# Five PSUM tiles from another set of banks, a recurrence in smaller steps, and memory attention ending later, in a one-core decoder step

## The chip, the cores and the metric

The kernel runs on one core of one Trainium2 chip. The core has five engines with queues of their own: PE multiplies matrices (PEld loads its weights), DVE and ACT work element by element, POOL issues a few transfers, and SP issues nearly all others. Each engine takes its instructions in the order in which the program wrote them into its queue; an instruction whose operands or whose target buffer are not ready holds up everything behind it on that engine. The metric is the device time of one execution in microseconds (us), as the median of several runs. A matrix product's result goes to one of eight banks of PSUM, each 128 partitions by 512 fp32 values.

## The reference

One inference step of a two-layer decoder (model width 1024, feed-forward width 2816), in fp32, for a prompt of 1024 tokens and for 8 "samples" of one token each that share all weights. Cut to what matters here:

```
layer 0:  q,f,i,g,qm = split(rmsnorm(x) @ w_in_a)
          k = 1 - exp(logf);  S = exp(logf)*S + k*v;   o = q @ S        # recurrence, 4 heads, state 128x128
          om = softmax(qm @ mem_k / sqrt(128)) @ mem_v                  # 4 heads, 256 memory tokens
          x += rmsnorm(concat(rmsnorm(o)*silu(g), om) @ w_o)
          x += rmsnorm((silu(h @ gate) * (h @ up)) @ w_down)            # h = rmsnorm(x)
shared K, V = split(rmsnorm(x) @ w_kv)
layer 1:  stick-breaking attention over K, V beside memory attention, w_o, then feed-forward
```

A prompt's memory is one of 256 tokens; each sample has a memory cache, a recurrent state and a paged K/V cache of its own, read from HBM. For a sample the recurrence is one step, `S = F*S + K*v; o = Q.S`, over 128x128 states of 4 heads and 8 samples, and the memory attention is a few vector products over 512 KB of keys and as many of values.

## The kernel before, in words

**Two groups.** Every projection runs in fp32 split into two halves: `split_w` (L198 to L212) loads a block of weights on SP (L203), ACT copies the high half (L208), DVE subtracts it to get the low half (L209), and `proj` (L214) multiplies three times: high by high, high by low, low by high (L222). PE can't start a group of such products before ACT and DVE have both served its weights. The loop `fw` (class `ffn_w`, `gate_up_w`, L578 for its products, L571 and L573 for its splits, L538 for its loads) forms a gate and an up product of the feed-forward together, with seven products of half size in place of eight; a block is one such set of seven. Part 3's fourth and last slice is such a block. Its raw loads and splits take buffers from the sample's pools in turn: here `raws` (L692) takes every second raw tile from `B()` (7 tiles of 256 KB), and `spl` (L680) takes three of every eight split tiles from `C()` (4 tiles of 512 KB).

**What sets the order.** `weave` (L178) advances several streams of code, each a Python generator; it always steps the one with the fewest steps divided by its weight, so a larger weight means that a stream's `yield`s come sooner. The order in which the streams' code runs is the order of the engines' queues, apart from `tc.issue_after(split[0].ins)`, which ties a DVE instruction to the place behind the last weight split's subtraction, in the order and not in time. A tile that is asked for while its pool is full waits for the oldest one's last reader.

**The streams that the change touches.** All tokens are in two groups: group 0 has 512 of the prompt, group 1 the other 512 and the 8 samples, hence tiles of 520 or 2 x 260 columns. `a1` is layer 0's mixer of group 1, `f0` layer 0's feed-forward of group 0. They run together in two stages:

```
weave((a1.sample(), 12), (a1.gate(), 4), (f0.part(1), 14), (w0, 9))
weave((chain(a1.merge(), a1.mem()), 27), (a1.mem_sample(), 82), (rest(), 33))
```

The first stage (about 505 to 618 us) has `hgrn_sample` (L1238): per head it loads a 512 KB state (`c<-in_state_hgrn`) and the values broadcast over the partitions (`c<-vd`, L1248), multiplies the state by F (L1272), the values by K (L1273), adds (L1274), stores, multiplies by Q (L1278) and lets PE sum over the partitions. Beside it `f0.part(1)` runs gate and up products (bias or Silu on DVE at L247 and L251, product at L819, split at L230) and then `w_down`. The second stage (618 to about 790 us) has `mem_attn_sample` (L1124): `sample_scores` (L1037) transposes the queries on PE (L1045), copies them to HBM (`qd`) and broadcasts them back (`b<-qd`, L1055), and per sample multiplies 512 KB of keys (L1057) and reduces (L1060); then the softmax (L1131 to L1144: PE transpose, DVE maximum L1133, ACT exponential L1136, DVE L1137 and L1138, PE transpose L1142, DVE copy L1144); then `sample_pv` (L1065), per sample a load of 512 KB of values (L1104), a product (L1080), a sum (L1083), a split, and PE's sum over the partitions (L1071, pairs), then the copy L1091 and four transposes L1095 with their splits (L229 on ACT, L230 on DVE). `a1.mem()` is the prompt's memory attention (L978, L991, L1010). `rest()` is feed-forward part 2, then `set_banks(True)` and parts 3 and 4 of `fw`.

**The banks.** `S()` (L121) rotates through three banks. `NS()` (L98) has a single one, and holds also the accumulated sum of `sample_pv` (L1066). The other four are two double banks for `proj` (`mm`), or, after `set_banks(True)`, four quadrants `q`.

Of the kernel before, what the change touches and what calls it, by code (L numbers as in the profile page):

```python
# [23 lines left out]
def tile_decoder(  # L24
# [6 lines left out]
    nc = tc.nc  # L31
# [66 lines left out]
    def NS():  # L98
        return nsp.tile([P, 512], F32, tag="ns", name=nm("ns"))
# [21 lines left out]
    def S():  # L121
        return smp.tile([P, 512], F32, tag="s", name=nm("s"))
# [51 lines left out]
    def chain(*gens):  # L174
        for g_ in gens:
            yield from g_

    def weave(*streams):  # L178

        live = [[0, n, g_] for g_, n in streams]  # L180
        while live:
            cur = min(live, key=lambda e: e[0] / e[1])
            cur[0] += 1
            try:
                next(cur[2])
            except StopIteration:
                live.remove(cur)
# [8 lines left out]
    split = [None]  # L196
# [840 lines left out]
    def sample_scores(q, load, sc):  # L1037
        qc = small([P, H * NB], tag="ss")
        for i in range(2):
            nc.vector.tensor_copy(  # L1040
                qc[:, i * 2 * NB : (i + 1) * 2 * NB].rearrange("p (h b) -> p h b", h=2), q[i][:, :, G : G + NB]
            )
        pq = S()
        for h in range(H):
            nc.tensor.transpose(pq[:NB, h * P : (h + 1) * P], qc[:, h * NB : (h + 1) * NB], ident)  # L1045
        qt = B()
        nc.vector.tensor_copy(qt[:NB, :], pq[:NB, :])
        qd = tc.dram_tile([NB, 512], F32, name=nm("qd"))
        nc.sync.dma_start(qd, qt[:NB, :])
        yield  # L1050
        scv = sc.rearrange("p (k h b) -> p k h b", k=2, h=H)
        for b in range(NB):
            kt = load(b)
            qb = B()
            nc.sync.dma_start(qb, qd[b].partition_broadcast(P))  # L1055
            with tc.issue_after(split[0].ins):
                nc.vector.tensor_mul(kt, kt, qb.unsqueeze(1).to_broadcast([P, 2, 512]))  # L1057
            yield
            with tc.issue_after(split[0].ins):
                nc.vector.tensor_reduce(  # L1060
                    scv[:, :, :, b], kt.rearrange("p k (h d) -> p k h d", h=H), axis=AX.X, op=ALU.add
                )
            yield

    def sample_pv(pT, load, xo, k0):  # L1065
        po = NS()  # L1066
        pv4 = pT.rearrange("p (k h b) -> p k h b", k=2, h=H)

        def total(b, parts):
            for i, p in enumerate(parts):  # L1070
                nc.tensor.matmul(  # L1071
                    po[:NB, :], selr[:, b, :], p, start=(b == 0 and i == 0), stop=(b == NB - 1 and i == 1)
                )

        late = None
        for b in range(NB):
            vt = load(b)
            v4 = vt.rearrange("p k (h d) -> p k h d", h=H)
            with tc.issue_after(split[0].ins):
                nc.vector.tensor_mul(v4, v4, pv4[:, :, :, b].unsqueeze(3).to_broadcast([P, 2, H, P]))  # L1080
            yield
            with tc.issue_after(split[0].ins):
                nc.vector.tensor_add(vt[:, 0, :], vt[:, 0, :], vt[:, 1, :])  # L1083
            new = b, halves(vt[:, 0, :], npool.tile([P, WID], F32R, tag="n", name=nm("n"))[:, :512], B(F32R))
            if late:
                total(*late)
            late = new
            yield
        total(*late)
        ot = B()  # L1090
        nc.vector.tensor_copy(ot[:NB, :], po[:NB, :])  # L1091
        yield
        pr = S()
        for h in range(H):
            nc.tensor.transpose(pr[:, h * NB : (h + 1) * NB], ot[:NB, h * P : (h + 1) * P], ident[:NB, :NB])  # L1095
        for h in range(H):
            d = xo[k0 + h]
            split_to((d[:, 0, G : G + NB], d[:, 1, G : G + NB]), pr[:, h * NB : (h + 1) * NB])
        yield
# [24 lines left out]
    def mem_attn_sample(l, qm, xo):  # L1124
        HB = H * NB
        sc = small([P, 2 * HB], tag="sc", bufs=2)
        yield from sample_scores(qm, mem_loader(cache_mem_k, l), sc)
        yield
        pr = S()
        for blk in range(2):  # L1130
            nc.tensor.transpose(pr[:HB, blk * P : (blk + 1) * P], sc[:, blk * HB : (blk + 1) * HB], ident)  # L1131
        nmx = small([P, 2], tag="nmx")
        nc.vector.tensor_reduce(nmx[:HB, 0:1], pr[:HB, :NM], axis=AX.X, op=ALU.max, negate=True)  # L1133
        sm = small([P, 2], tag="sme")
        pe = B()
        nc.scalar.activation(pe[:HB, :NM], pr[:HB, :NM], AF.Exp, bias=nmx[:HB, 0:1], accum_out=sm[:HB, 0:1])  # L1136
        nc.vector.reciprocal(sm[:HB, 0:1], sm[:HB, 0:1])  # L1137
        nc.vector.tensor_scalar(pe[:HB, :NM], pe[:HB, :NM], sm[:HB, 0:1], None, op0=ALU.mult)  # L1138
        yield
        pb = S()  # L1140
        for blk in range(2):
            nc.tensor.transpose(pb[:, blk * HB : (blk + 1) * HB], pe[:HB, blk * P : (blk + 1) * P], ident[:HB, :HB])  # L1142
        pT = small([P, 2 * HB], tag="ss")
        nc.vector.tensor_copy(pT, pb[:, : 2 * HB])  # L1144
        yield
        yield from sample_pv(pT, mem_loader(cache_mem_v, l), xo, H)
# [91 lines left out]
    def hgrn_sample(Ft, Kt, Qt, vd):  # L1238
# [25 lines left out]
        for h in range(H):  # L1264
            def col(t):
                return t[h // 2][:, h % 2, G : G + NB].unsqueeze(2).to_broadcast([P, NB, P])

            st, vb = nxt
            nxt = h < H - 1 and fetch(h + 1)
            stv, vbv = (t.rearrange("p a (b v) -> p (a b) v", v=P) for t in (st, vb))  # L1270
            with tc.issue_after(split[0].ins):
                nc.vector.tensor_mul(stv, stv, col(Ft))  # L1272
            nc.vector.tensor_mul(vbv, vbv, col(Kt))  # L1273
            nc.vector.tensor_add(st, st, vb)  # L1274
            nc.sync.dma_start(st_sample[0, :, h].rearrange("b k v -> k b v"), stv)
            total()
            yield
            nc.vector.tensor_mul(vbv, stv, col(Qt))  # L1278
            for a in range(2):
                qs = B(F32R), B(F32R)  # L1280
                split_to(qs, vb[:, a, :])
                late.extend((h, a, i, p) for i, p in enumerate(qs))
            yield
# [9 lines left out]
        pr = S()  # L1293
# [300 lines left out]
    def sb_sample(Qs, xo):  # L1594
# [5 lines left out]
        e = small([P, 2 * HB], tag="ss")  # L1600
        softplus(zb, e, 2 * HB)
        yield
        cu = S()
        nc.tensor.matmul(cu[:, 0:HB], trif, e[:, 0:HB], start=True, stop=False)
        nc.tensor.matmul(cu[:, 0:HB], ones, e[:, HB : 2 * HB], start=False, stop=True)
        nc.tensor.matmul(cu[:, HB : 2 * HB], trif, e[:, HB : 2 * HB], start=True, stop=True)
# [137 lines left out]
    a1 = mixer_a(1, x1)  # L1744
# [6 lines left out]
    f0 = ffn(0, 0, o0.x)  # L1751
    weave((a1.core(), 22), (f0.part(0), 14), (islice(w0, 16), 17))
    a1.open()
    weave((a1.sample(), 12), (a1.gate(), 4), (f0.part(1), 14), (w0, 9))

    def rest():
        yield from f0.part(2)
# [3 lines left out]
        yield from fw.part(4)  # L1761
        f0.acc = fw.acc

    weave((chain(a1.merge(), a1.mem()), 27), (a1.mem_sample(), 82), (rest(), 33))
    xk0, xb0 = [], []
    o1 = out_proj(1, 0, M)
    drain(o1.mm(a1.xo, 0, 1, True))
# [81 lines left out]
```

## Time and profile before

| | |
|---|---|
| median of 3 runs | 2410.87 us (2408.98 to 2412.88) |
| profiled execution, its own time | 2413.43 us |
| span of its records | 2411.6 us |
| PE busy | 2379.0 us, 99% of the span |
| DVE busy | 1734.8 us, 72% |
| ACT busy | 1283.5 us, 53% |
| mean granted PE clock | 0.998 |
| PE idle in the span | 32.6 us |

Of the 32.6 us in which PE was not busy 10.2 lie in two waits at the very start. A timeline row gives the start in us from the start of the span, the duration, engine, line, operation and the names written and read, the count, and in brackets how long the engine stood idle before it and what released it. A waits row has the total, the number and the longest. A windows row has the window, its length, the busy times and counts of PE, PEld, DVE, ACT and POOL, PE's clock and the share and GB/s of the DMA engines. A row of transfers has what is moved, the queue, the count, the KB of each, and the median us from its issue to its landing. Names with `ws` are split weights, `w` and `b<-in_w_gu`, `b<-wsum` raw ones, `mm`, `s`, `ns` and `q` are PSUM tiles of the sets above, and `c` is a 512 KB tile.

### The profile page before, as it was taken

The numbers are of one execution on the slowest core, as the hardware profiler recorded it, in microseconds if no ns is written. First come the engines' busy times: TensorE is split into PE (matmuls) and PEld (weight loads), VectorE is DVE, ScalarE is ACT, GpSimd is POOL, SyncE is SP. The second block draws the span as 40 slices with busy tenths as digits, with TensorE's granted clock in tenths as the row PEclk, the third lists the DMA queues.
The fourth block names the chain that finished last, engine by engine and source line by source line (L and its number), as shares of the span: only waits on it lengthen the run. The fifth ranks groups of instructions, "written<-read, shape, count | busy, mean of one in ns | idle before, by whom it ended". The sixth has DMA issues, their size and how long they took to land.

```text
span 2411.6 us, 42315 instructions
## 1 busy us (share of the span) xinstructions
PE 2379.0 (99%) x15959; PEld 2156.3 (89%) x15959; DVE 1734.8 (72%) x3220; ACT 1283.5 (53%) x2559; POOL 113.2 (5%) x187
## 2 busy tenths in 40 slices
PE   8999999999999999999999999999999999999998
PEld 6888989888789998999999989877778899999998
DVE  5867558666896676879666777778787679776866
ACT  5547544444454554667544554556454466554445
POOL 1000202100000000000001200111000000000000
PEclk9999999999999999999999999999999999999999
DMA  6454766566644447432568846545353354343342
GB/s 189 123 167 111 173 194 163 132 187 181 203 140 136 146 139 217 124 112 81 163 176 218 230 141 190 173 137 157 109 157 118 99 160 136 105 130 100 109 128 76
DMA packets 510991, 357.59 MB, mean 148 GB/s; under 512 B 20109, under 2 KB 459514, under 8 KB 510786
## 3 DMA queue, kind: packets, MB, share of 16 engines
q1 hardware_dynamic: 494914, 312.93, 43.6%
q0 software_dynamic: 15872, 41.95, 7.5%
q8 instruction: 126, 2.06, 0.4%
q14 instruction: 79, 0.65, 0.1%
HBM read 322.86 MB, written 65.49 MB: 161 GB/s over the span
## 4 chain that ended last, share of the span: by engine, by line
PE 51%; DVE 2%; ACT 2%; DMA 1%; issue 1%; DVEq 0%; SPq 0%; ACTq 0%
PE mm L222 17%; PE q L578 16%; PE q L750 10%; PE q L504 1%; PE s L1565 1%; PE s L1525 1%; PE q L782 1%; PE s L1010 1%; PE s L991 1%; PE s L1554 1%; DMA w<-in_w_in_b 0%; DVE x L230 0%; PE ns L1071 0%; PE s L978 0%; PE s L504 0%
## 5 line engine op out<-in xcount | busy, mean ns | idle before, releaser
L222 PE MATMUL mm<-x,ws 128*128 128x512 f32 (+1 forms) x5016 | 925.5, 342 | 5.3 <-DVE ws L209 1.5
L222 PEld LDWEIGHTS mm<-x,ws 128*128 128x128 f32 x5016 | 774.5, 188 | 115.9 <-issue 3.9
L208 ACT CAST ws<-w 128x512 fp32r<-128x512 f32 x596 | 347.9, 585 | 435.5 <-PE mm L222 254.4
L209 DVE TENSOR_TENSOR ws<-w,ws 128x512 fp32r<-128x512 f32 x596 | 380.9, 645 | 227.2 <-ACT ws L208 224.2
L750 PE MATMUL q<-m,ws 128*128 128x260 f32 (+1 forms) x2496 | 304.2, 282 | 0.4 <-DVE m L230 0.2
L750 PEld LDWEIGHTS q<-m,ws 128*128 128x128 f32 x2496 | 299.7, 188 | 1.6 <-ACT m L229 0.7
L578 PE MATMUL q<-y,ws 128*128 128x260 f32 (+1 forms) x1920 | 249.6, 284 | 0.5 <-ACT q L586 0.5
L578 PEld LDWEIGHTS q<-y,ws 128*128 128x128 f32 x1920 | 237.8, 189 | 1.6 <-ACT q L586 0.7
L578 PE MATMUL q<-x,ws 128*128 128x260 f32 (+1 forms) x1668 | 220.4, 283 | 3.0 <-ACT ws L571 1.6
L578 PEld LDWEIGHTS q<-x,ws 128*128 128x128 f32 x1668 | 207.8, 188 | 4.4 <-ACT ws L571 2.2
L222 PE MATMUL mm<-m,ws 128*128 128x512 f32 x768 | 187.2, 397 | 0.0
L571 ACT CAST ws<-w 128x512 fp32r<-128x512 f32 x206 | 125.1, 619 | 96.3 <-PE q L750 30.7
L573 DVE TENSOR_TENSOR ws<-w,ws 128x512 fp32r<-128x512 f32 x206 | 139.5, 688 | 44.7 <-ACT ws L571 43.4
L222 PEld LDWEIGHTS mm<-m,ws 128*128 128x128 f32 x768 | 142.5, 188 | 31.3
L759 DVE TENSOR_TENSOR r<-r,q 128x260 f32<-128x260 f32 (+1 forms) x160 | 60.6, 420 | 48.7 <-PE q L750 48.6
L504 PE MATMUL q<-x,ws 128*128 128x260 f32 (+1 forms) x720 | 87.1, 282 | 0.0
L504 PEld LDWEIGHTS q<-x,ws 128*128 128x128 f32 x720 | 86.4, 188 | 0.2
L229 ACT CAST m<-t 128x512 fp32r<-128x512 f32 (+1 forms) x88 | 54.8, 623 | 49.0 <-DVE t L819 26.9
L571 ACT CAST ws<-b 128x512 fp32r<-128x512 f32 x82 | 50.5, 620 | 39.2 <-PE q L750 13.4
L573 DVE TENSOR_TENSOR ws<-b,ws 128x512 fp32r<-128x512 f32 x82 | 56.4, 688 | 17.8 <-ACT ws L571 15.9
L230 DVE TENSOR_TENSOR m<-t,m 128x512 fp32r<-128x512 f32 (+1 forms) x88 | 60.8, 691 | 11.2 <-ACT m L229 10.4
L277 DVE TENSOR_TENSOR st<-st,n 128x512 f32<-128x512 f32 (+1 forms) x91 | 62.2, 691 | 4.0 <-ACT n L276 2.7
(410 smaller groups left out, 3092.0 us busy)
## 6 DMA issues: line engine op xcount, KB each, us to landing
w<-in_w_gu SPq DMA_DIRECT2D x275, 256.0 KB, 3.3
w<-in_w_down SPq DMA_DIRECT2D x160, 256.0 KB, 3.0
wsum<-in_w_gu POOLq DMA_DIRECT2D x48, 512.0 KB, 6.0
w<-in_w_in_a SPq DMA_DIRECT2D x80, 256.0 KB, 3.0
w<-in_w_o SPq DMA_DIRECT2D x64, 256.0 KB, 3.0
w<-wsum SPq DMA_DIRECT2D x61, 256.0 KB, 3.1
b<-in_w_gu SPq DMA_DIRECT2D x39, 256.0 KB, 4.0
b<-wsum SPq DMA_DIRECT2D x39, 256.0 KB, 3.3
```

Of the source, the lines that this page charges most:

```text
L208: nc.scalar.copy(ws[:, 0, :n, :], raw[:, :n, :])
L209: split[0] = nc.vector.tensor_sub(ws[:, 1, :n, :], raw[:, :n, :], ws[:, 0, :n, :].bitcast(F32))
L222: nc.tensor.matmul(ps[:, a, : PW[g]], wt, xt[k][:, xi, o : o + PW[g]], start=(k == 0 and wi == 0), stop=(k == nk - 1 and wi == 2),)
L229: nc.scalar.copy(dst[0], src)
L230: nc.vector.tensor_sub(dst[1], src, dst[0].bitcast(F32))
L277: nc.vector.tensor_add(acc[:, :n], acc[:, :n], t[:, :n])
L504: ins = nc.tensor.matmul(pp[a][:, :h], wt, xt[k][:, xi, a * h : (a + 1) * h], start=(k == 0 and wi == 0), stop=(k == ND - 1 and wi == 2),)
L571: nc.scalar.copy(w[:, 0, :], src)
L573: split[0] = nc.vector.tensor_sub(w[:, 1, :], src, w[:, 0, :].bitcast(F32))
L578: nc.tensor.matmul(ps[:, :h], w[:, wj, k * P : (k + 1) * P], x[:, xi, :], start=(first and k == 0 and wi == 0), stop=(k == 3 and wi == 2), ...
L750: nc.tensor.matmul(pp[a][:, :h], wt, mids[k][:, xi, a * h : (a + 1) * h], start=(k == 0 and wi == 0), stop=(k == nf - 1 and wi == 2),)
L759: nc.vector.tensor_add(d, d, pp[a][:, :h])
```

## The change

Five tiles move from `S()` to `NS()`: the transpose of the samples' queries (`pq`), the transposes of the scores and of the probabilities in `mem_attn_sample` (`pr`, `pb`), the transpose of its result (`pr` of `sample_pv`) and the sum `cu` of stick-breaking. The recurrence of `hgrn_sample` gets one more `yield` per head, and L1273 and L1278 are placed behind the last weight split by `issue_after`, which was so for L1272 alone. In the first stage the weight of `a1.sample()` goes from 12 to 16, for it has more steps; in the second the weight of `a1.mem_sample()` goes from 82 to 70. Nothing is computed differently, and each engine has as many instructions as before. After it every line from the old L1273 on is moved by 2 or 3: L1273 is L1275, L1274 is L1276, L1278 is L1281, L1295 is L1298.

```diff
 def sample_scores(q, load, sc):
-        pq = S()
+        pq = NS()
 def sample_pv(pT, load, xo, k0):
         ot = B()
         nc.vector.tensor_copy(ot[:NB, :], po[:NB, :])
         yield
-        pr = S()
+        pr = NS()
 def mem_attn_sample(l, qm, xo):
-        pr = S()
+        pr = NS()
...
-        pb = S()
+        pb = NS()
 def hgrn_sample(Ft, Kt, Qt, vd):
             with tc.issue_after(split[0].ins):
                 nc.vector.tensor_mul(stv, stv, col(Ft))
-            nc.vector.tensor_mul(vbv, vbv, col(Kt))
+            yield
+            with tc.issue_after(split[0].ins):
+                nc.vector.tensor_mul(vbv, vbv, col(Kt))
             nc.vector.tensor_add(st, st, vb)
             nc.sync.dma_start(st_sample[0, :, h].rearrange("b k v -> k b v"), stv)
             total()
             yield
-            nc.vector.tensor_mul(vbv, stv, col(Qt))
+            with tc.issue_after(split[0].ins):
+                nc.vector.tensor_mul(vbv, stv, col(Qt))
 ...
-        cu = S()
+        cu = NS()
 ...
-    weave((a1.sample(), 12), (a1.gate(), 4), (f0.part(1), 14), (w0, 9))
+    weave((a1.sample(), 16), (a1.gate(), 4), (f0.part(1), 14), (w0, 9))
...
-    weave((chain(a1.merge(), a1.mem()), 27), (a1.mem_sample(), 82), (rest(), 33))
+    weave((chain(a1.merge(), a1.mem()), 27), (a1.mem_sample(), 70), (rest(), 33))
```

The first place is DVE's queue in the first stage, where the second head's state is multiplied. Before:

```order
L1272 TENSOR_TENSOR c_5362<-c_5362,a_2293 128x1024
L1273 TENSOR_TENSOR c_5467<-c_5467,a_2495 128x1024
L819 TENSOR_TENSOR t_5313<-t_5313,mm_5332 128x512
L1274 TENSOR_TENSOR c_5362<-c_5362,c_5363 128x1024
L230 TENSOR_TENSOR m_5358<-t_5313,m_5358 128x512
L209 TENSOR_TENSOR ws_5480<-w_5478,ws_5480 128x512
L209 TENSOR_TENSOR ws_5485<-w_5483,ws_5485 128x512
L1278 TENSOR_TENSOR c_5363<-c_5362,a_2692 128x1024
L247 TENSOR_SCALAR t_5408<-mm_5383 128x512
```

After, with L1275 the product that was L1273:

```order
L1272 TENSOR_TENSOR c_5323<-c_5323,a_2293 128x1024
L819 TENSOR_TENSOR t_5313<-t_5313,mm_5338 128x512
L209 TENSOR_TENSOR ws_5473<-w_5471,ws_5473 128x512
L230 TENSOR_TENSOR m_5364<-t_5313,m_5364 128x512
L209 TENSOR_TENSOR ws_5478<-w_5476,ws_5478 128x512
L247 TENSOR_SCALAR t_5408<-mm_5383 128x512
L209 TENSOR_TENSOR ws_5538<-w_5536,ws_5538 128x512
L251 TENSOR_TENSOR t_5409<-t_5409,t_5408 128x512
L209 TENSOR_TENSOR ws_5543<-w_5541,ws_5543 128x512
L1275 TENSOR_TENSOR c_5324<-c_5324,a_2294 128x1024
L1276 TENSOR_TENSOR c_5323<-c_5323,c_5324 128x1024
L819 TENSOR_TENSOR t_5409<-t_5409,mm_5434 128x512
```

Before, the values' product L1273 that stands right behind the second head's L1272 is that of the third head (tile `c_5467`), and L819 stands behind it. After, it is the product of the same head (`c_5324`, added to the state `c_5323` at L1276), it stands nine rows later behind four weight splits, and L819 stands right behind L1272.

The second place is PE's queue in the second stage, at the samples' softmax. Before:

```order
L222 MATMUL mm_6631<-x_4077,ws_6628 128x512 x3
L1131 MATMUL s_6660<-ident,sc_6231 32x128 x2
L1010 MATMUL s_6670<-c_6493,a_3798 128x256 x2
L978 MATMUL s_6682<-ident,b_6607 128x128 x4
L222 MATMUL mm_6702<-m_6328,ws_6699 128x512 x2
L991 MATMUL s_6689<-b_6618,c_6494 128x256 x2
L222 MATMUL mm_6702<-m_6328,ws_6699 128x512
L222 MATMUL mm_6702<-m_6432,ws_6699 128x512 x3
L222 MATMUL mm_6702<-m_6545,ws_6699 128x512 x2
L1142 MATMUL s_6692<-ident,b_6666 128x32 x2
L222 MATMUL mm_6702<-m_6545,ws_6699 128x512
```

After, with the two transposes in `ns`:

```order
L222 MATMUL mm_6706<-m_6651,ws_6703 128x512 x3
L1131 MATMUL ns_6720<-ident,sc_6231 32x128 x2
L1010 MATMUL s_6730<-c_6487,a_3798 128x256 x2
L978 MATMUL s_6742<-ident,b_6665 128x128 x4
L991 MATMUL s_6678<-b_6676,c_6488 128x256 x2
L222 MATMUL mm_6763<-m_6328,ws_6760 128x512 x3
L1142 MATMUL ns_6753<-ident,b_6726 128x32 x2
L222 MATMUL mm_6763<-m_6427,ws_6760 128x512 x3
L222 MATMUL mm_6763<-m_6539,ws_6760 128x512 x3
```

Between the first transpose (L1131) and the second (L1142) stand 16 products (two of L1010, four of L978, two of L991, eight of L222) before and 11 (three of L222) after.

The third place is SP's queue before part 3's last block, whose seven weights are the L538 rows. Before:

```order
L1104 DMA c_7355<-in_cache_mem_v 128x2x512
L538 DMA w_7645<-wsum_2369 128x4x128
L203 DMA w_7686<-in_w_down 128x4x128
L203 DMA w_7719<-in_w_down 128x4x128
L538 DMA b_7548<-in_w_gu 128x4x128
L538 DMA b_7587<-wsum_2367 128x4x128
L538 DMA b_7624<-wsum_2368 128x4x128
L538 DMA b_7663<-in_w_gu 128x4x128
L538 DMA b_7972<-wsum_3669 128x4x128
L538 DMA b_8007<-in_w_gu 128x4x128
```

After:

```order
L203 DMA w_7686<-in_w_down 128x4x128
L203 DMA w_7719<-in_w_down 128x4x128
L538 DMA b_7511<-in_w_gu 128x4x128
L1104 DMA c_7546<-in_cache_mem_v 128x2x512
L203 DMA w_7752<-in_w_down 128x4x128
L1104 DMA c_7636<-in_cache_mem_v 128x2x512
L538 DMA b_7560<-wsum_2367 128x4x128
L538 DMA b_7597<-wsum_2368 128x4x128
L203 DMA w_7785<-in_w_down 128x4x128
L203 DMA w_7818<-in_w_down 128x4x128
L538 DMA b_7650<-in_w_gu 128x4x128
L538 DMA b_7972<-wsum_3669 128x4x128
```

Before, all eight values loads (`c<-in_cache_mem_v`) are past, and the four L538 loads of the block that go to `b` tiles stand in a row. After, the last two values loads stand among them: one right behind the block's first raw load, the other behind one `w_down` load and ahead of the raw loads of the block's third and fifth products, `b_7560` and `b_7597`.

The same place on PE, before:

```order
L1071 MATMUL ns_6735<-n_7326,selr 8x512
L1071 MATMUL ns_6735<-b_7327,selr 8x512
L1071 MATMUL ns_6735<-n_7511,selr 8x512
L1071 MATMUL ns_6735<-b_7512,selr 8x512
L978 MATMUL s_7521<-ident,b_7338 128x128 x4
L991 MATMUL s_7528<-b_7349,c_6494 128x256 x2
L1095 MATMUL s_7531<-ident,b_7519 128x8 x4
L578 MATMUL q_7545<-a_7009,ws_7568 128x256 x2
L991 MATMUL s_7528<-b_7526,c_6494 128x256 x2
L578 MATMUL q_7544<-x_3792,ws_7550 128x256 x3
L578 MATMUL q_7544<-x_3860,ws_7550 128x256 x3
```

After, where the block begins and where its sixth product ends:

```order
L578 MATMUL q_7507<-x_3792,ws_7513 128x256 x3
L578 MATMUL q_7507<-x_3860,ws_7513 128x256 x3
L578 MATMUL q_7507<-x_3867,ws_7513 128x256 x3
L578 MATMUL q_7507<-x_3934,ws_7513 128x256 x3
L578 MATMUL q_7508<-a_6989,ws_7531 128x256 x4
L578 MATMUL q_7508<-a_7249,ws_7531 128x256 x6
L578 MATMUL q_7507<-x_3938,ws_7580 128x256 x2
L1071 MATMUL ns_6796<-n_7550,selr 8x512
L1071 MATMUL ns_6796<-b_7551,selr 8x512
L578 MATMUL q_7509<-a_6987,ws_7562 128x256 x3
L578 MATMUL q_7509<-a_7096,ws_7562 128x256 x3
```

```order
L578 MATMUL q_7510<-x_4006,ws_7620 128x256 x3
L578 MATMUL q_7510<-x_4013,ws_7620 128x256 x3
L578 MATMUL q_7510<-x_4077,ws_7620 128x256 x3
L1071 MATMUL ns_6796<-n_7640,selr 8x512
L1071 MATMUL ns_6796<-b_7641,selr 8x512
L1095 MATMUL ns_7673<-ident,b_7648 128x8 x4
L578 MATMUL q_7509<-a_6988,ws_7652 128x256 x2
L750 MATMUL q_7691<-m_7110,ws_7688 128x256
L750 MATMUL q_7692<-m_7110,ws_7688 128x256
```

Before, both last pairs of L1071 and the four transposes L1095 stand ahead of the block (`q_7544`, first weight `ws_7550`). After, the pair of the seventh sample stands behind the block's second product and the first two rows of its fourth (`ws_7580`), and ahead of its third (`ws_7562`); the pair of the eighth stands with L1095 behind the sixth (`ws_7620`), right ahead of the seventh's first row (`ws_7652`).

## The prediction

> **What bounds the kernel now.** First the page's line of busy times, then the waits of PE over the whole span, the largest first.
>
> ```profile
> PE 2379.0 (99%) x15959; PEld 2156.3 (89%) x15959; DVE 1734.8 (72%) x3220; ACT 1283.5 (53%) x2559; POOL 113.2 (5%) x187
> ```
>
> ```profile
> PE ns L363 <- DVE xtok L336: 10.2, 2, 7.9
> PE s L1565 <- issue: 3.3, 2, 1.7
> PE s L1554 <- ACT b L1548: 1.8, 4, 0.7
> ```
>
> PE is busy for 2379.0 of 2411.6 us. The change removes no product, so all that it can move is in the 32.6 us in which PE stands. The 10.2 at the start are out of its reach; some 22 are left, and a gain is bounded by what of these lies in the places that the change touches. A loss has no such bound: PE has no slack, so any operand that now comes late is paid in full. Next, the waits between 480 and 800 us, where the two changed stages lie, and the busy times of two windows in them.
>
> ```profile
> PE mm L222 <- DVE t L819: 1.5, 1, 1.5
> PE q L578 <- ACT ws L571: 1.3, 1, 1.3
> PE mm L222 <- DVE t L247: 1.2, 1, 1.2
> PE mm L222 <- DVE ws L209: 0.5, 1, 0.5
> PE q L578 <- DVE ws L573: 0.3, 1, 0.3
> ```
>
> ```profile
> 660.00:720.00 60.00, 60.00 (x341) 50.88 (x340) 56.89 (x114) 32.89 (x74) 0.00 (x0) 1.00 0.47 140
> 720.00:780.00 60.00, 58.43 (x460) 56.33 (x459) 39.81 (x85) 30.14 (x61) 0.00 (x0) 0.97 0.48 137
> ```
>
> In these 300 us PE waits 4.7 us, five times. From 660 to 720, where the samples' attention runs at its thickest, it waits for nothing, though DVE is busy for 56.89 of 60 us (the third busy time in the row): there is no gain to be had there, and little room.
>
> **The recurrence in steps (first stage): -2.7 us.** DVE's timeline around the second and third heads, and PE's:
>
> ```profile
> 523.63 1.22 DVE L1272 TENSOR_TENSOR c<-c,a 128x1024 f32<-128x1024 f32 x1
> 528.62 1.23 DVE L1273 TENSOR_TENSOR c<-c,a 128x1024 f32<-128x1024 f32 x1 [3.77 <-DMA c<-vd]
> 529.77 0.68 DVE L819 TENSOR_TENSOR t<-t,mm 128x512 f32<-128x512 f32 x1
> ...
> 547.79 1.23 DVE L1273 TENSOR_TENSOR c<-c,a 128x1024 f32<-128x1024 f32 x1 [4.43 <-DMA c<-vd]
> 548.93 0.69 DVE L247 TENSOR_SCALAR t<-mm 128x520 f32<-128x520 f32 x1
> ```
>
> ```profile
> 530.59 0.70 PE L222 MATMUL mm<-x,ws 128*128 128x512 f32 x2 [1.48 <-DVE t L819]
> ```
>
> L1273 multiplies the values of a head that is not due yet; it stands on DVE at the place where it was free to go in the order, and waits 3.77 and 4.43 us for their load. L819 and L247 queue behind it; they free the double bank that PE wants next, and PE stands for 1.48 us and 1.18 us (1.2 in the waits). After the change the product stands nine rows behind L1272 of its own head, whose values' load was issued a head earlier (the two waits lie 19.2 us apart, a head's time), so that it has landed and L819 comes right behind L1272. Both gaps go: 1.48 + 1.18 = 2.66. Nothing has to be paid for it on DVE, since the products are the same, at 1.22 each, and DVE idled 3.77 and 4.43 us there. The new `yield`s put L1276 and L1281, 1.22 each, between weight splits as well; three such products back to back are 3.7 us, which the idle time given back covers. Between 0 (a split behind L1275 is late in its place) and -2.66 I take -2.66.
>
> **Samples' scores and softmax (start of the second stage): +3.2 us.** The transposes L1045 now stand inside the first projection of part 2, ten products (each 17.36/74 = 0.23 us below) behind its start, and the samples' tail and the merge stand ahead of the scores on DVE.
>
> ```profile
> 620.77 17.36 PE L222 MATMUL mm<-x,ws 128*128 128x512 f32 x74
> 638.59 1.66 PE L222 MATMUL mm<-x,ws 128*128 128x512 f32 x6 [0.46 <-DVE ws L209]
> ```
>
> ```profile
> 628.12 2.36 DVE L1057 TENSOR_TENSOR c<-c,b 128x1024 f32<-128x1024 f32 x2 [0.82 <-DMA b<-qd]
> ```
>
> So each L1057 comes some 2.4 us later against PE, and with it the L209 splits and the L247 and L819 that were placed behind it. In the old order one split in this stretch was late already (0.46). Sixteen score products of 1.2 us stand between the splits. From below the cost is 0, as in the window from 660 to 720, where a DVE at 95% hid it all; from above it is two gaps like the largest that a queue on DVE made, 2 x 1.48 = 3.0. I take 2.0, nearer to the upper end, because the one gap that there was lies on this very queue. Then the softmax:
>
> ```profile
> 668.15 0.38 PE L1131 MATMUL s<-ident,sc 128*32 128x128 f32 x2
> 668.36 1.03 PE L1010 MATMUL s<-c,a 128*128 128x256 f32 x4
> 669.23 0.60 PE L978 MATMUL s<-ident,b 128*128 128x128 f32 x4
> ...
> 672.71 0.31 PE L1142 MATMUL s<-ident,b 32*128 32x32 f32 x2
> ```
>
> ```profile
> 671.15 0.33 DVE L1138 TENSOR_SCALAR b<-b,sme 32x256 f32<-32x256 f32 x1
> ```
>
> From L1131's end (668.53) to the end of L1138 (671.48), which L1142 needs, the chain took 2.95 us, hidden under 16 products. Now 11 stand there: two of L1010 and two of L991 at 0.26 each, four of L978 at 0.15, three of L222 at 0.23: 2.3 us. PE then waits 0.7 at least, and 1.9 if L1142 needs all of the 4.2 us that lay between the two ends; I take 1.2. Together 2.0 + 1.2 = 3.2, between 0.7 and 4.9. The tile `ns` costs nothing by itself: it is free until the values' sum begins, which needs L1144 anyway.
>
> **Memory attention's end inside part 3's last block: +7 us.** Before, on SP, PE, ACT and DVE:
>
> ```profile
> 738.50 0.37 SPq L538 DMA_DIRECT2D b<-in_w_gu  x1
> 741.82 0.92 SPq L538 DMA_DIRECT2D b<-wsum  x2
> ```
>
> ```profile
> 741.16 0.40 PE L1071 MATMUL ns<-n,selr 128*8 128x512 f32 x1
> ...
> 743.49 0.41 PE L1095 MATMUL s<-ident,b 8*128 8x8 f32 x4
> ...
> 746.46 0.50 PE L578 MATMUL q<-x,ws 128*128 128x256 f32 x2 [1.26 <-ACT ws L571]
> 747.27 1.45 PE L578 MATMUL q<-x,ws 128*128 128x256 f32 x10 [0.31 <-DVE ws L573]
> ```
>
> ```profile
> 742.29 0.68 DVE L1091 COPY b<-ns 8x512 f32<-8x512 f32 x1 [0.30 <-PE ns L1071]
> 744.93 0.17 DVE L230 TENSOR_TENSOR x<-s,x 128x8 fp32r<-128x8 f32 x1 [0.23 <-ACT x L229]
> ```
>
> ```profile
> 745.77 0.63 ACT L571 CAST ws<-b 128x512 fp32r<-128x512 f32 x1
> ```
>
> ```profile
> b<-in_w_gu SPq DMA_DIRECT2D x39, 256.0 KB, 4.0
> b<-wsum SPq DMA_DIRECT2D x39, 256.0 KB, 3.3
> c<-in_cache_mem_v SPq DMA_DIRECT2D x16, 512.0 KB, 4.2
> ```
>
> The block's raw loads were issued 4.6 to 8 us ahead of its first product at 746.46. After, the eighth values load stands on SP ahead of the third product's raw load (`b_7560`), and its 512 KB tile is the one that the first product's split weight holds, a tile of the same pool. It can't be issued before that product's last matmul; the raw load behind it waits as long. From there: one issue (0.46) and the load's landing (3.3), then the cast (0.63): 4.4 us, and the low half (0.3 more, as at 747.27). On PE stand, up to that product, ten matmuls (1.45), two more (0.3) and a pair of L1071 (0.40 each and overlapping, some 0.5): 2.2. PE waits 4.4 + 0.3 - 2.2 = 2.5, between 0 (the tile is freed sooner than I read) and 3.9 (the landing of 4.0 and the larger load of 4.2 in front); I take 3.0, since the larger load is under way. [...]
>
> Then the end. Before, L1091 (0.68), the four L1095 and four rounds of ACT and DVE on them (743.49 to 745.10, 1.6 us) ran while PE had L991 and others to do, and only the weight cast behind them on ACT (745.77) held PE, 1.26 + 0.31 us. After, the last pair of L1071 stands directly ahead of L1095, and the seventh product's first rows directly behind: PE waits for the copy (0.68 + 0.1), then through the rounds (1.6 less the 0.41 of L1095) and the cast of the seventh weight that stands behind them on ACT (0.63): 0.8 + 1.2 + 0.6 = 2.6. The next split weight, `ws_7688`, is cast behind that one: 0.63 more. From below it is 0.8, if ACT's casts are done between the rounds. The old wait at 746.46 stays as it is: the prompt's last L991, its cast and then the first weight's cast stand there as before (1.57). For the operands of the seventh sample's pair, whose values load goes out with the block's first raw load, I add one DVE row, 0.7. Sum 3.0 + 2.6 + 0.63 + 0.7 = 7, between 3 (the load's wait halved, the end at its 0.8, the rest nothing, and some of the old 1.57 kept) and 9.
>
> The bank for `cu` and the others in the later weave change next to nothing in the order, and cost nothing: the two waits at L1565 are not for banks,
>
> ```profile
> 1553.58 1.21 DVE L1060 TENSOR_REDUCE sc<-c 128x8 f32<-128x1024 f32 x1
> 1554.70 0.74 DVE L1540 TENSOR_SCALAR b<-s,biasp 128x512 f32<-128x512 f32 x1
> 1555.55 0.48 DVE L1562 MEMSET s<- 128x512 f32 x1
> ```
>
> but for the MEMSET of their target, which DVE ran without a pause behind L1060 and L1540 and PE followed. That queue stays.
>
> **Sum.** -2.66 + 3.2 + 7 = +7.5. On the profiled execution's own 2413.43 us (span 2411.6) that is 2420.9; that execution lay 2.56 above the median of 2410.87, so the median forecast is 2410.87 + 7.5 = 2418.4.
>
> **Rivals.** *The raw load comes in time.* If the eighth values load goes out before the first product's end, the third product isn't late, and +7 becomes +4; with the scores at 1.9 in place of 3.2 the sum is -2.66 + 1.9 + 4 = +3.2: 2414.1. For it: at 741.82 SP was 4.6 us ahead of PE's use at 746.46. Against it: a tile's reuse is a wait that no early issue goes round.
>
> *Banks are what PE waits for (the other side).* Three `s` banks serve the prompt's attention, the samples' and stick-breaking; five tiles fewer in their rotation could end the waits at L1565 (3.3) and L1554 (1.8), with the first stage's 2.66: -7.8, 2403.1. It decides if the second stage costs less than 3.0, for then the net passes 4.8. [...] Against it stands the MEMSET on DVE, which follows its queue and not a bank's release, and L1554's releaser, ACT.
>
> *The block's delay spreads.* Part 4's raw loads stand on SP behind the block's last one and come 7 us later in wall time; if PE catches up with them, one more landing of 3.3 us is paid: +10.8, 2421.7. Against it: w_down's 32 products lie between.
>
> **How the numbers follow.** A measurement of this kernel can tell about 0.2%, 4.8 us, from no change. My forecast has 0.50, the spread 0.14, the raw load in time 0.22, the banks 0.09, and 0.05 is left for a first stage that gains while the second costs 0 to 2 (2408 to 2410). Slower by over 0.2% (above 2415.7) hold the forecast and the spread, and some of the third case: 0.65; the same: 0.25; faster (below 2406.05): 0.10. With every term at its low end (-2.66 + 0.7 + 3) the forecast's own sum is 2411.9, with every one at its high end (0 + 4.9 + 9) it is 2424.8; since they won't all be there together, 2413 to 2423 is the likeliest case's own range. The range from 2409 to 2424 takes in the case of the raw load and most of the spread, and leaves out the banks.
>
> **What would show it.** Right: no wait of PE behind L819 or L247 near 530 and 549; a wait at L1142 of about 1 us; in the last block a wait for ACT `ws` L571 or DVE `ws` L573 of about 3 us at its third product, behind a `b<-wsum` load that was issued after the first product, and 2 to 3 us around L1095. The order of the loads on SP shows the second of these most clearly. Wrong: the same `b<-wsum` loads issued before the first product; a window from 720 to 780 with PE at 58 or more; or waits at L1565 gone. The prediction fails most easily on the third product's wait, its largest term, and next on the scores, which no row of the old trace prices.

## The result and the profile after

The changed kernel takes 2421.62 us (median of 6 runs, 2419.33 to 2423.04) against 2411.64 us of the kernel before on the same chip: a ratio of 1.0038, 95% interval 1.0028 to 1.0048. It is slower by 10.0 us; 7.5 were forecast. Its profiled execution took 2422.14 us, with a span of 2420.4, which is 8.8 more than before.

First the page's busy times after, then what PE waited for between 480 and 810 us.

```profile
PE 2384.2 (99%) x15959; PEld 2161.7 (89%) x15959; DVE 1735.2 (72%) x3220; ACT 1282.6 (53%) x2559; POOL 112.2 (5%) x187
```

```profile
PE q L578 <- ACT ws L571: 6.6, 3, 3.4
PE ns L1095 <- DVE b L1091: 0.8, 1, 0.8
PE ns L1142 <- ACT b L1021: 0.6, 1, 0.6
PE mm L222 <- DVE ws L209: 0.4, 1, 0.4
PE ns L1071 <- DVE b L230: 0.3, 1, 0.3
PE q L578 <- DVE ws L573: 0.3, 1, 0.3
PE ns L1071 <- ACT n L229: 0.3, 1, 0.3
```

The waits here grew from 4.7 to 9.2 us, summed before rounding: +4.5. Those in the first 60 us are 0.9 shorter, which the change doesn't touch; the other differences cancel. The same 15959 matmuls were busy for 5.2 us longer. 4.5 - 0.9 + 5.2 = 8.8.

L819 and L247 no longer appear: the two gaps of the recurrence are gone. In the place of the first, on DVE:

```profile
522.13 1.22 DVE L1272 TENSOR_TENSOR c<-c,a 128x1024 f32<-128x1024 f32 x1
523.31 0.69 DVE L819 TENSOR_TENSOR t<-t,mm 128x512 f32<-128x512 f32 x1
...
532.89 1.22 DVE L1275 TENSOR_TENSOR c<-c,a 128x1024 f32<-128x1024 f32 x1
534.14 1.22 DVE L1276 TENSOR_TENSOR c<-c,c 128x1024 f32<-128x1024 f32 x1
```

L819 follows L1272 at once, and L1275 comes 10.8 us behind it without a wait for its load. Nearly all of the new waits are in part 3's last block. On SP, ACT and PE:

```profile
734.53 0.37 SPq L538 DMA_DIRECT2D b<-in_w_gu  x1
734.95 0.50 SPq L1104 DMA_DIRECT2D c<-in_cache_mem_v  x1
743.57 0.37 SPq L203 DMA_DIRECT2D w<-in_w_down  x1
744.52 0.37 SPq L1104 DMA_DIRECT2D c<-in_cache_mem_v  x1
744.99 0.96 SPq L538 DMA_DIRECT2D b<-wsum  x2
```

```profile
749.98 0.62 ACT L571 CAST ws<-b 128x512 fp32r<-128x512 f32 x1 [3.92 <-DMA b<-wsum]
```

```profile
743.00 1.45 PE L578 MATMUL q<-x,ws 128*128 128x256 f32 x10 [0.30 <-DVE ws L573]
...
746.11 0.40 PE L1071 MATMUL ns<-n,selr 128*8 128x512 f32 x1 [0.25 <-ACT n L229]
746.84 0.40 PE L1071 MATMUL ns<-b,selr 128*8 128x512 f32 x1 [0.33 <-DVE b L230]
750.65 3.23 PE L578 MATMUL q<-a,ws 128*128 128x256 f32 x12 [3.41 <-ACT ws L571]
...
760.18 0.41 PE L1095 MATMUL ns<-ident,b 8*128 8x8 f32 x4 [0.77 <-DVE b L1091]
762.55 0.53 PE L578 MATMUL q<-a,ws 128*128 128x256 f32 x2 [1.96 <-ACT ws L571]
```

The eighth values load goes out at 744.52, when the first product (743.00 and 1.45 long) has ended; the third product's raw load behind it goes out at 744.99, its cast starts at 749.98, and PE waits 3.41 us. The end of the memory attention then holds PE for 0.77 and 1.96 us. Together with the operands of L1071 (0.25 and 0.33) that is 6.72 us.

The 5.2 us of longer products are mostly the clock. Windows of 4 us, after and then before; the first number behind the last bracket is PE's granted clock, 1.00 for the full one:

```profile
748.00:752.00 4.00, 1.35 (x5) 1.13 (x6) 1.38 (x3) 1.24 (x2) 0.00 (x0) 0.65 0.43 128
752.00:756.00 4.00, 4.00 (x20) 4.00 (x20) 2.95 (x4) 0.37 (x1) 0.00 (x0) 0.50 0.58 172
...
764.00:768.00 4.00, 4.00 (x27) 4.00 (x27) 2.99 (x6) 2.24 (x5) 0.00 (x0) 0.71 0.57 165
```

```profile
748.00:752.00 4.00, 4.00 (x24) 4.00 (x23) 3.89 (x7) 2.94 (x6) 0.00 (x0) 0.57 0.70 206
```

From 752 to 756 only 20 products ran in 4 us, at a clock of 0.50; in the kernel before 36 ran in these 4 us, at 1.00. Summed in windows of 0.1 us (PE's busy time by the clock that is missing) the stretches at a clock of 0.50, slow stretches from here on, cost 6.1 us after, 2.7 and 1.7 of them behind the two waits of the block and 1.7 near 1566, and 1.7 before: +4.4 of the +5.2. The last 0.8 is not assigned. The stretch near 1566 follows a wait of 1.80 us at L1568, which was 1.70 before (then L1565), without such a stretch; so 2.7 of the 4.4 belong to the block.

### The profile page after: what moved, and what is told of

Its sections match the earlier page's. It is cut to its first block, busy times and chain, and to the rows that moved or that the text cites. A ratio compares the mean times of both kernels' runs of the same rounds, so it can differ in the third digit from the quotient of the medians.

```text
span 2420.4 us, 42315 instructions
## 1 busy us (share of the span) xinstructions
PE 2384.2 (99%) x15959; PEld 2161.7 (89%) x15959; DVE 1735.2 (72%) x3220; ACT 1282.6 (53%) x2559; POOL 112.2 (5%) x187
## 4 chain that ended last, share of the span: by engine, by line
PE 50%; DVE 2%; ACT 2%; DMA 1%; issue 1%; SPq 0%; DVEq 0%; ACTq 0%
PE mm L222 16%; PE q L578 16%; PE q L750 10%; PE q L504 1%; PE s L1568 1%; PE q L782 1%; PE s L1528 1%; DMA b<-qd 1%; PE s L1010 1%; PE s L991 1%; PE s L1557 0%; DMA w<-in_w_in_b 0%; DVE ws L209 0%; DVE x L230 0%; PE ns L1071 0%
## 5 line engine op out<-in xcount | busy, mean ns | idle before, releaser
L222 PE MATMUL mm<-x,ws 128*128 128x512 f32 (+1 forms) x5016 | 926.0, 342 | 2.8 <-DVE ws L209 1.7
L222 PEld LDWEIGHTS mm<-x,ws 128*128 128x128 f32 x5016 | 775.9, 189 | 112.6 <-DVE ws L209 2.7
L209 DVE TENSOR_TENSOR ws<-w,ws 128x512 fp32r<-128x512 f32 x596 | 381.3, 645 | 234.4 <-ACT ws L208 228.8
L578 PE MATMUL q<-y,ws 128*128 128x260 f32 (+1 forms) x1920 | 249.7, 284 | 0.5 <-ACT q L586 0.5
L578 PEld LDWEIGHTS q<-y,ws 128*128 128x128 f32 x1920 | 237.7, 189 | 1.6 <-ACT q L586 0.7
L578 PE MATMUL q<-x,ws 128*128 128x260 f32 (+1 forms) x1668 | 221.7, 284 | 3.0 <-ACT ws L571 1.6
L578 PEld LDWEIGHTS q<-x,ws 128*128 128x128 f32 x1668 | 208.9, 189 | 4.3 <-ACT ws L571 2.2
L222 PE MATMUL mm<-m,ws 128*128 128x512 f32 x768 | 186.7, 397 | 0.0
L573 DVE TENSOR_TENSOR ws<-w,ws 128x512 fp32r<-128x512 f32 x206 | 139.5, 688 | 45.1 <-ACT ws L571 43.0
L222 PEld LDWEIGHTS mm<-m,ws 128*128 128x128 f32 x768 | 142.9, 188 | 31.6
L573 DVE TENSOR_TENSOR ws<-b,ws 128x512 fp32r<-128x512 f32 x82 | 56.4, 688 | 22.0 <-ACT ws L571 21.4
```

The lines of the kernel that those rows point to most:

```text
L209: split[0] = nc.vector.tensor_sub(ws[:, 1, :n, :], raw[:, :n, :], ws[:, 0, :n, :].bitcast(F32))
L222: nc.tensor.matmul(ps[:, a, : PW[g]], wt, xt[k][:, xi, o : o + PW[g]], start=(k == 0 and wi == 0), stop=(k == nk - 1 and wi == 2),)
L573: split[0] = nc.vector.tensor_sub(w[:, 1, :], src, w[:, 0, :].bitcast(F32))
L578: nc.tensor.matmul(ps[:, :h], w[:, wj, k * P : (k + 1) * P], x[:, xi, :], start=(first and k == 0 and wi == 0), stop=(k == 3 and wi == 2), ...
```

## The experiments

**Which part of the change costs the time?** Three runs take it apart.

```diff
-    weave((chain(a1.merge(), a1.mem()), 27), (a1.mem_sample(), 70), (rest(), 33))
+    weave((chain(a1.merge(), a1.mem()), 27), (a1.mem_sample(), 82), (rest(), 33))
```

> The changed kernel with the second stage's weight back at 82; steps and banks stay. If the loss is the end of the memory attention inside part 3's block (its waits of 6.7 us and the slower clock behind them), all of it goes and the first stage's 2.7 us stay: 2408 to 2410 us, with no wait over 1.6 us between 720 and 790. If banks or the samples' tail ahead of the scores cost time, 2412 to 2416.

Measured: 2411.10 us against 2412.50, ratio 0.9994 (0.9985 to 1.0003), between the two expected ranges. The loss is gone, and with it all waits over 1.6 us between 480 and 800; but the gain of 2.7 isn't there in full, for PE now waits 1.39 us near 640, where it waited 0.46.

```diff
-    weave((chain(a1.merge(), a1.mem()), 27), (a1.mem_sample(), 82), (rest(), 33))
+    weave((chain(a1.merge(), a1.mem()), 27), (a1.mem_sample(), 70), (rest(), 33))
```

> The kernel before with the weight 70 and nothing else. If the weight alone makes the loss, 2411.6 plus 6.7 of waits, plus 3 to 4 for the clock, without the first stage's gain: 2421 to 2424 us, with waits of about 3.4 and 2.7 us in the block and the gaps at 530 and 549 still there. If it takes the new banks as well, below 2417.

Measured: 2421.70 us, ratio 1.0037 (1.0023 to 1.0050), as much as the whole change. The waits of this kernel between 480 and 800 us:

```profile
PE q L578 <- ACT ws L571: 5.6, 3, 2.5
PE mm L222 <- DVE t L819: 1.8, 1, 1.8
PE s L1095 <- DVE b L1091: 0.8, 1, 0.8
```

The number 70 alone makes the loss; steps and banks aren't needed for it. The two gaps of the recurrence aren't fixed sizes: the first stage is that of the kernel before, and they are 1.77 and 0.19 us here, where they were 1.48 and 1.18.

```diff
             with tc.issue_after(split[0].ins):
                 nc.vector.tensor_mul(stv, stv, col(Ft))
+            yield
+            with tc.issue_after(split[0].ins):
                 nc.vector.tensor_mul(vbv, vbv, col(Kt))
...
-    weave((a1.sample(), 12), (a1.gate(), 4), (f0.part(1), 14), (w0, 9))
+    weave((a1.sample(), 16), (a1.gate(), 4), (f0.part(1), 14), (w0, 9))
```

> The kernel before with the recurrence in steps and the weight 16, and nothing else. By the forecast's first term the gaps of 1.48 and 1.18 us go and nothing comes for them: 2408.5 to 2409.5 us. If the samples' tail, now later, pushes the scores into weight splits (the forecast's 2.0), 2411 or more, with new waits for L209 splits near 640.

Measured: 2411.70 us, ratio 0.9995 (0.9986 to 1.0004). The waits between 480 and 800 us:

```profile
PE mm L222 <- DVE ws L209: 1.5, 1, 1.5
PE q L578 <- ACT ws L571: 1.3, 1, 1.3
PE q L578 <- DVE ws L573: 0.3, 1, 0.3
```

Both gaps of the recurrence went, 2.66 us, but the one at 640 grew from 0.46 to 1.50: the forecast's term for the scores is real, at half its size, once the first stage is faster. With the weight 70 it isn't there (0.42 after): on DVE one split L209 stands ahead of the fourth L1057 instead of behind it.

**Do banks matter?** The five tiles alone, in the kernel before:

```diff
-        pq = S()
+        pq = NS()
...
-        cu = S()
+        cu = NS()
```

> The kernel before with the five tiles in the other set and nothing else. By the forecast they cost and bring nothing: within 0.5 us of the kernel before. By the rival, that PE waits for banks, the waits at L1565 and L1554 (5.1 us) go: 2406 to 2408.

Measured: 2411.46 us against 2410.93, ratio 1.0002 (0.9993 to 1.0011). The rival that PE waits for banks in the kernel before falls; the waits behind the MEMSET are still there (1.80 and 1.00 at L1565).

**Is it the place of the values load on SP?** The eighth load goes to POOL's queue instead:

```diff
-            nc.sync.dma_start(t, src[l, b].rearrange("(k p) h d -> p k (h d)", p=P))
+            q = nc.gpsimd if src is cache_mem_v and l == 0 and b == NB - 1 else nc.sync
+            q.dma_start(t, src[l, b].rearrange("(k p) h d -> p k (h d)", p=P))
```

> The changed kernel with the eighth sample's values load issued by POOL instead of SP, so that the raw load behind it on SP need not wait for the tile. The w_down load ahead of both was itself issued only at 743.57, so the raw load can come 1.0 us sooner by its place and up to 1.6 us sooner by a landing of 3.3 instead of 4.9: the wait of 3.4 falls to between 0.8 and 2.4, and the time by 1 to 2.6 us, plus 0 to 2.7 for the slow clock behind it: 2417 to 2420.5. If the landing, not the turn on SP, is the cause, it stays within 0.5 us of 2421.6.

Measured: 2416.71 us, ratio 1.0018 (1.0009 to 1.0027): 4.9 us less than the changed kernel, a little more than expected. SP, POOL and ACT of this kernel (L1105 is L1104 of the changed one):

```profile
744.17 0.37 SPq L203 DMA_DIRECT2D w<-in_w_down  x1
744.70 0.94 SPq L538 DMA_DIRECT2D b<-wsum  x2
```

```profile
745.34 0.78 POOL L1105 DMA_DIRECT2D c<-in_cache_mem_v  x1 [145.15 <-DVE c L1080]
```

```profile
747.68 0.62 ACT L571 CAST ws<-b 128x512 fp32r<-128x512 f32 x1 [1.03 <-DMA b<-wsum]
751.63 0.62 ACT L571 CAST ws<-b 128x512 fp32r<-128x512 f32 x1 [3.34 <-DMA b<-wsum]
```

The raw load now goes out right behind the w_down load, and its cast starts 3.0 us later; after the change that took 5.0 (744.99 to 749.98). The wait of 3.41 shrank to 0.52, and the clock behind it stays at 1.00. The turn on SP cost about 1 us (from the w_down load's issue to the raw load's it is 0.53 here and was 1.42), and the 512 KB that travelled in front of the raw load about 2. What is left is put down to the w_down load, which in the changed kernel waited 8.0 us for a buffer of its own (released by L573 on DVE); no run moves that load. Nor is the 512 KB load's price gone: it now holds the raw load of the fifth product, whose cast starts at 751.63, and PE waits 0.87 us behind that cast. So the block's waits fall only from 6.72 to 5.5 us. In the profiled executions the slow stretch behind the first wait (2.7) is gone, the one behind the second is 6.8 us long instead of 3.4 and costs 1.1 more, and the one near 1566 (1.7) isn't there.

**Is the second wait the chain of copy, transposes, rounds and cast?** The four transposes are tied behind the block's last product:

```diff
         ot = B()
         nc.vector.tensor_copy(ot[:NB, :], po[:NB, :])
         yield
+        wait = k0 == H and not ended
+        if wait:
+            ended.append(1)
+            for _ in range(2):
+                yield
         pr = NS()
         for h in range(H):
-            nc.tensor.transpose(pr[:, h * NB : (h + 1) * NB], ot[:NB, h * P : (h + 1) * P], ident[:NB, :NB])
+            with tc.issue_after(prod[0].ins) if wait else ExitStack():
+                nc.tensor.transpose(pr[:, h * NB : (h + 1) * NB], ot[:NB, h * P : (h + 1) * P], ident[:NB, :NB])
```

> The changed kernel with the last four transposes (L1095) and their splits tied behind the block's last product, so that the seventh product no longer stands behind copy, transposes, rounds and cast. The waits of 0.77 and 1.96 us go, and the clock at 0.5 behind them (1.55 us lost) with them: 2421.6 - 4.3 = 2417.3, or 2418.9 where the clock stays. If the seventh product's raw load is late itself (issued at 753.61), most of the 1.96 stays: 2420 to 2421.

Measured: 2417.89 us, ratio 1.0022 (1.0014 to 1.0031): 3.7 us less. The wait of 0.77 is gone, that of 1.96 is 1.00, and there is no slow stretch behind it (the one behind the first wait, 2.86 here, stays and costs 2.9). What is left of it isn't the raw load: the seventh cast stands on ACT behind L618, and that waits 2.41 us for a sum on DVE (L615) which reads the sixth product (line numbers of the changed kernel).

**Does the slow clock follow from the pause?** Ten products that nobody reads fill the long wait; they compute nothing that is used:

```diff
+            if b == 6 and not filled:
+                filled.append(1)
+                fill = S()
+                for _ in range(10):
+                    with tc.issue_after(mm.ins):
+                        nc.tensor.matmul(fill[:NB, :], selr[:, b, :], p, start=True, stop=True)
```

> The changed kernel with ten extra products of 0.23 us, whose result nobody reads, right behind the seventh sample's L1071 pair, where PE stood for 3.41 us. They lie inside the wait and delay nothing. If the clock at 0.5 from 749.4 to 756 follows from PE standing still before, about 2.7 us of it go, and the time falls to about 2419 though PE does more: 2418.5 to 2420. If the clock doesn't depend on the pause, the time stays at 2421.6 or grows by up to 1.

Measured: 2418.74 us, ratio 1.0024 (1.0015 to 1.0033): 2.9 us less with more work on PE. In this kernel, PE and the windows (the extra products are at L1080, and L579 is L578 of the changed kernel):

```profile
746.22 2.45 PE L1080 MATMUL s<-b,selr 128*8 128x512 f32 x10
749.86 0.50 PE L579 MATMUL q<-a,ws 128*128 128x256 f32 x2 [1.19 <-ACT ws L572]
```

```profile
748.00:752.00 4.00, 2.59 (x17) 1.80 (x16) 2.16 (x4) 1.24 (x2) 0.00 (x0) 1.00 0.13 39
752.00:756.00 4.00, 4.00 (x36) 3.97 (x35) 3.19 (x5) 1.64 (x4) 0.00 (x0) 1.00 0.82 243
...
760.00:764.00 4.00, 4.00 (x23) 3.93 (x23) 2.99 (x6) 3.06 (x7) 0.00 (x0) 0.60 0.51 147
```

The third product comes no sooner than without the filling (5.25 us behind the fourth product's first rows, 744.61 to 749.86, where it was 5.19, 745.46 to 750.65), but the clock stays at 1.00 where it was 0.65 and 0.50. The stretch behind the second wait, which wasn't filled, is still there (0.60).

**Is it the lateness, or the places?** Other weights in the changed kernel, each an edit of the one number: 74, 78 and 90.

> The changed kernel with the weight 74: the memory attention still ends inside the block, but the eighth values load takes a tile that nothing in the block holds, and L1095 stands ahead of the third product instead of ahead of the seventh. The w_down load ahead of the raw load stays, so that load goes out near 744 as with the load on POOL. By the theory of places one wait is left ahead of the third product, about 2.5 to 4 us in all (operands of the pair, copy, rounds and cast, which now overlap the raw load's landing), with none ahead of the seventh, and the 0.4 at 640 as with 70: 2412.5 to 2416 us. If ending inside the block costs by itself, 2419 or more.

Measured: 2415.96 us, ratio 1.0013 (1.0004 to 1.0022). Its waits in the block:

```profile
PE q L578 <- ACT ws L571: 1.2, 1, 1.2
PE ns L1071 <- ACT n L229: 1.1, 1, 1.1
PE ns L1095 <- DVE b L1091: 0.8, 1, 0.8
```

With the 0.33 ahead of the second L1071 that is 3.35 us, half of 6.72, though the memory attention ends in the block here too. The slow stretch behind these waits costs 2.8 us, as much as the one behind the first wait of the changed kernel.

> The changed kernel with the weight 78: on SP all eight values loads stand ahead of the block's raw loads to b tiles, and the pairs and L1095 ahead of its first product. By the account of the loss, nothing of the block's 6.7 us is left, and the samples' scores press on the weight splits less than at 82 (a gap of 1.4 at 639 there, 0.4 at 70): 2408 to 2410.5 us, 0 to 1 under the one with 82. If the loss grows with the lateness as such and not with the place of the loads, it lies between the two, near 2415.

Measured: 2409.88 us against 2412.70, ratio 0.9988 (0.9979 to 0.9996): faster than both kernels. One wait is left between 480 and 800 us:

```profile
PE mm L222 <- DVE ws L209: 1.5, 1, 1.5
```

The old wait of 1.57 at the block's first product is gone as well, which I hadn't expected: the first weight's cast (741.29) no longer stands on ACT behind the rounds of L1095 (from 743.47) and the cast for the prompt's last L991 (743.53), but ahead of both.

> The changed kernel with the weight 90: memory attention's end is ahead of the block altogether, so that the first product's cast has no rounds ahead of it on ACT: the wait of 1.57 us near 744 should shrink to under 0.8, and the scores press more: the gap near 639 is 1.4 or more. 2408 to 2411 us.

Measured: 2414.88 us, ratio 1.0011 (1.0002 to 1.0019). The gap at 641 is 2.37 us, with a slow stretch behind it that costs 1.7, and the wait at the first product is still 1.49 (1.19 and 0.30): the forecast of under 0.8 fails. An earlier end crowds the scores; it doesn't free the first product's cast, which here stands on ACT behind the cast for the prompt's last L991. The profiled execution took 2412.23; what the slower runs add isn't shown.

The places of 78 with the old banks:

> The kernel before with the recurrence in steps and the weight 78, with the old banks. If the banks do nothing, 2409 to 2411 us as the weight 78 with the new ones had. If the third bank matters at the end of the memory attention, where L1095 stands close to the prompt's L991, the wait of 1.2 to 1.6 us ahead of the first product is back: 2411 to 2413.

Measured: 2408.41 us against 2410.93, ratio 0.9991 (0.9982 to 1.0000), within the noise the same as with the new ones. There is no wait ahead of the first product, but the trace has one for a bank: L1131 waits 1.02 us for ACT's L1021, which reads an `s` tile. With the new banks and the weight 78 that wait isn't there; the medians don't show it. And 80 with an empty step, to have the scores of 70 and the end of 78:

```diff
-    weave((chain(a1.merge(), a1.mem()), 27), (a1.mem_sample(), 70), (rest(), 33))
+    ms = a1.mem_sample()
+    weave((chain(a1.merge(), a1.mem()), 27), (chain(islice(ms, 3), [None], ms), 80), (rest(), 33))
```

> The changed kernel with the weight 80 for the samples' memory attention and one empty step put behind its third step. At the scores the order on DVE is that of 70 (one split L209 ahead of the fourth L1057), at the end that of 78 (values loads ahead of the block's raw loads, pairs and L1095 ahead of its first product). If the two gaps found are places in the order and nothing else, neither the 1.4 to 1.55 us at 640 nor the block's 6.7 come: 1.1 under the weight 78, 2407.5 to 2409.5 us. If the earlier end takes the gap at 640 along, it equals the weight 78.

Measured: 2410.85 us against 2410.93, ratio 1.0001 (0.9992 to 1.0010): a miss. The gap at 640 is gone, but another one comes:

```profile
PE ns L1131 <- DVE sc L1060: 2.2, 1, 2.2
```

The last scores are late for the softmax's transpose. So in the orders tried with this early end, the scores' work on DVE held PE at one end or at the other.

## Why the prediction was right

The sign, the place of the loss and the size of its largest term came out as forecast; the time lies within the stated range, 3.2 us above the forecast 2418.4. The steps one by one:

- **The recurrence, -2.66.** Both gaps went as worked out. The steps alone bring little, for 1.0 comes back at 640.
- **Scores, +2.0.** This step failed: 0.42 after against 0.46 before. "So each L1057 comes some 2.4 us later against PE" overlooked that the weight 70 also moves the L1057s behind splits in the order. At 82 the term is there, with 1.0.
- **Softmax, +1.2.** 0.55, below its lower bound of 0.7, at the place named: L1138 ended at 676.38 and L1142 started at 676.53, though the waits row names ACT's L1021. The price of the 11 products was too low: each of L1010 and L991 in the order is two records in the timeline (1.03 us for four), so that 2.9 us lay between the transposes, not 2.3.
- **The third product, +3.0.** 3.41. The tile's wait was as read (744.52, behind the first product's end; SP waited 0.5 us for a product of L578 there). Two sizes were off and offset each other, which is luck: the cast came 5.0 us behind the issue, not 3.3, since the 512 KB load travelled in front; and a w_down load that waited for its own buffer held SP until 743.57 anyway, so that the turn itself cost only 1 us (the load on POOL). The 0.7 for the pair's operands were 0.58.
- **The end, +2.6 and 0.63.** 0.77 + 1.96 = 2.73, with nothing at the split weights behind it: the casts (762.40 to 764.58) ran while PE was busy with the seventh product, and PE had no wait behind 762.55.
- **Left out: the clock.** The sum of the waits, 6.72 in the block against 6.9 forecast, is nearly exact, yet the products behind both long pauses ran at a clock of 0.50, and the slow stretches cost 4.4 us more than before, 2.7 of it in the block (filling the long wait made the kernel 2.9 faster). No term stood for it, though the trace of before had such a stretch from 748 to 752. The scores and the softmax, 2.7 us too dear together, hid most of the omission in the sum: that the total came so near is luck.

Of the rivals, banks (the five tiles alone) and the raw load in time (its issue at 744.99) fell. The third, that the delay spreads, had the number 2421.7, almost the one measured, but not by its mechanism: from 763 to 810 PE doesn't wait at all, so no further landing was paid.

## What to carry to other kernels

A load on a shared queue costs what stands behind it: a load that must wait for its tile holds every raw load behind it, and when it goes its bytes travel in front of theirs (here about 1 us and about 2); look up which later instruction the tile's last reader is before a stream is moved. A weight in a round robin isn't a speed: 70, 74, 78, 82 and 90 gave 1.0038, 1.0013, 0.9988, 0.9994 and 1.0011, so each value is to be read from the order it makes. Where PE is the bound, a pause can cost more than its length, by the clock behind it: the wait of 3.41 us was followed by 6.83 us at 0.50, which cost another 2.7.

## What the runs showed of the hardware

In the 14 traces, without the first 20 us and the end, the stretches at a clock of 0.50 were 3.41 or 6.83 us long: one such unit with PE busy cost 1.7 us, two cost 2.7 to 3.1. They sit on a grid, by the clock's records in the traces. In the changed kernel the clock changes at 749.23, 756.06, 762.89 and 766.30: 2, 4 and 5 times 3.413 us behind the first. With the weight alone it changes at 745.03, 748.44, 751.86, 755.27, 762.10 and 768.92: 1, 2, 3, 5 and 7 times 3.413 behind the first.

On this grid the pauses can be read. In the same traces a window of this grid in which PE stood for 1.89 us or more (1.89 with the weight back at 82, 2.58 and 2.67 in the changed kernel) had one at 0.50 behind it; of those with 1.5 to 1.85 some had (1.57 in the kernel before, 1.80 in the changed one) and some hadn't (1.70 before, from 1554.12 to 1557.53, and 1.84 with the empty step); those with less (1.48 in the changed kernel) had none, except where the clock was at 0.50 already (1.41 there, from 749.23). So a pause that a boundary divided could be harmless here. The same 1.57 us at the block's first product, in rows of windows cut on the grid, before and then with the weight back at 82:

```profile
745.17:748.59 3.42, 1.85 (x14) 1.62 (x14) 2.74 (x6) 3.36 (x8) 0.00 (x0) 1.00 0.86 214
748.59:752.00 3.41, 3.41 (x19) 3.41 (x18) 3.30 (x6) 2.35 (x5) 0.00 (x0) 0.50 0.82 242
```

```profile
741.40:744.81 3.41, 2.15 (x13) 1.53 (x12) 1.63 (x7) 2.09 (x8) 0.00 (x0) 1.00 0.97 269
744.81:748.23 3.42, 3.11 (x27) 2.98 (x26) 3.42 (x7) 3.42 (x9) 0.00 (x0) 1.00 0.66 189
```

Before, all of it lies in one window, and the next is at 0.50. With the weight back at 82 a boundary divides it into 1.26 and 0.31, and the clock stays at 1.00. In the kernel with the empty step, pauses of 2.19 and 2.58 us are divided into 1.84 and 0.35, and 1.08 and 1.50, and no slow stretch follows either. What else decides between 1.5 and 1.85 isn't shown.

In two traces (the kernel before, and the steps alone) 1.57 us of standing in a window of 3.41 were followed by a clock of 0.50: PE had worked in the rest of it.
